# Cross-attention values as three F32R passes, and a later load of the final norm's weights, in a hybrid decoder layer

## The chip, the core and the metric

The kernel runs on one core of one Trainium2 chip. The core has five engines with instruction streams of their own: TensorE (PE; its weight loads are shown as PEld), VectorE (DVE), ScalarE (ACT), GpSimd (POOL) and SyncE (SP). SP only issues transfers here; POOL issues the transfers that add to what already stands in SBUF. Each engine takes its instructions in order. The metric is the device time of one execution in microseconds, as the median of several runs; one execution was also taken by the hardware profiler, and all lines of the profile are from that one.

## The reference

One decoder layer, `x` of 256 x 1024 in float32, with three gated branches (A: causal attention of 6 heads, B: a gated MLP that mixes tokens, C: cross attention of 4 heads into 256 memory tokens), then a final norm. What matters here is branch C and the end:

```python
def memory_cross_attention(q, mem_n, w_mem_kv):
    mk, mv = jnp.split(mem_n @ w_mem_kv, 2, axis=-1)
    ...
    lg = jnp.einsum('bshd,bmhd->bhsm', qh, kh).astype(jnp.float32) * (HEAD_DIM ** -0.5)
    p = jax.nn.softmax(lg, axis=-1).astype(q.dtype)
    return jnp.einsum('bhsm,bmhd->bshd', p, vh).reshape(B, S, C_WIDTH)
...
    out_c = memory_cross_attention(qc, mem_n, w_mem_kv[layer]) * jax.nn.silu(gc)
    y = (jax.nn.sigmoid(ma) * (out_a @ w_branch_a[layer])
         + jax.nn.sigmoid(mb) * (out_b @ w_branch_b[layer])
         + jax.nn.sigmoid(mc) * (out_c @ w_branch_c[layer]))
    x = x + y @ w_out[layer]
return rms_norm(x, final_norm_g)
```

## The kernel before

**Chunks.** The weights stream through in pieces of 128 x 1024 float32, called chunks. Each is split into a rounded high part (`split_hi`, ACT, line 264) and the rest (`split_lo`, VectorE, line 267), both in the type F32R; TensorE then makes three passes, high by high, high by low and low by high (`mm3`, lines 450 to 453). Five split chunks fit at a time (`SPL`), and a chunk is split four chunks ahead of its use (`LEAD`).

**The order of chunks** stands in `SEQUENCE` (line 52), which `plan` reads. A name such as `qc0`, `ga3` or `ub4` is a feature chunk (`mm_fea`), `w02` a branch chunk (`mm_br`, half 0, part 2), and a dot is the next product of `st`, which is two chunks of half the TensorE time each. Ahead of them come the memory's keys and values (`mm_mvk`) and a token chunk (`mm_tok`); behind them eight chunks of the output projection (`mm_out`). `n_br` is the number of chunks before those eight.

**The products of `st`** (`mm_st`) are in five groups. In a group seven products stand for eight: their left operands are sums and differences of the normed input, and their weights are sums of blocks. `ORDER` is the order of the seven, 1, 2, 5, 3, 6, 7, 4. The sums of weights are made in two buffers, `form0` and `form1`. Products 1, 2 and 3 load a block with a plain transfer from SP (`form_load`, line 231); products 5, 7 and 4 add a block onto what stands there, with a transfer from POOL (`form_add`, line 234); product 6 adds the two buffers on VectorE (`form_sum`, line 238). A transfer into a half of a buffer can go out once that half's last split is done; so 5 follows 1, 7 follows 3, 4 follows 6, 3 follows 2, and the next group's 2 and 1 follow 4 and 7.

**Plain weights** are loaded by SP, two chunks at a time, into three buffers `raw` (`load_part`, line 210).

**Everything else** is a list of units (`Units`) with an engine, a length, what each comes after, and sometimes a due chunk. Before and after every chunk `slot` issues the units that fit by a reckoned clock: one for TensorE goes out when what it needs is reckoned to be done 1.8 us before; one for another engine when that engine is reckoned free; one that is due goes out in any case. A unit without an engine, such as a load, goes out as soon as all that it comes after is issued. The order is so fixed when the kernel is built.

**Cross attention.** `evict_mv` (line 607) scales the values out of PSUM into the third part of `cx`, in float32. `join_half` makes high and low parts of the queries (`qch`, `qcl`) and keys (`mkh`, `mkl`) in the slots `och`, `sg0`, `ocl` and `sg1`. Per head h there is a chain of units: scores (`cs`, with `mm3`), the softmax (`cn`), the transpose of the probabilities and their copy to SBUF (`cp`: `c_pT` on TensorE, `c_pT_out` on ACT, line 918), then the product with the values and its copy (`cv`: `c_pv`, line 925, float32; `c_out`, line 931). `cp` of a head comes after `cv` of the head two before, `cs` after `cp` of the head three before; the six heads of branch A follow in the same row. None of these has a due chunk.

**Slots.** `slot_tile` puts a tile into a named place of SBUF; a later tile of the same name waits until all readers of the earlier one are done. `sg0` and `sg1` later hold the first gates (`sig0`, `sig1`), `ga` and `gc` the gates of branches A and C, then `ah` and a part of `al`; `ga` holds at the end the final norm's weights.

**The final norm's weights** (`load_fin`, line 771) are one transfer on SP of a row of 1024 to all 128 partitions, 512 KB. The unit `fin` comes after chunk `at_br[1, 2]`, the last that multiplies with `ah`, whose slot they take. `out_gain` (line 1140, POOL) multiplies with them in the output stage. `load_x` is issued eight chunks before the output chunks.

Of the kernel before, what the change touches and what calls it, by code (L numbers as in the profile page):

```python
# [24 lines left out]
F32 = mybir.dt.float32  # L25
F32R = mybir.dt.float32r
BF16 = mybir.dt.bfloat16
AF = mybir.ActivationFunctionType
# [5 lines left out]
S = 256  # L34
KD = D // 128
HA, GB, HC = 6, 6, 4
AW, BW, CW = 768, 768, 512
# [11 lines left out]
FAST = 5  # L49


SEQUENCE = ("qc0 . qc1 qc2 qc3 . q0 k0 . q1 . . k1 q2 . k2 q3 k3 . . q4 k4 . . q5 k5 . . ga0 ga1 . ga2 ga3 . . "
            "ga4 ga5 . . gc0 . gc1 . gc2 gc3 . ub4 ub5 . . gb4 gb5 . . w00 w01 . . w10 w11 . w02 w12 . . w03 w04 "
            ". . w05 w13 . . w14 w15 . w06 w07 . w16 w17")


# [21 lines left out]
PE, DVE, ACT, POOL, QUEUE = range(5)  # L78
# [69 lines left out]
def tile_hybrid_layer(ctx: ExitStack, tc: tile.TileContext, mw, xT, mem, x, fin_g, ln_g, w, ws, w_sp, b_sp, b_spt, rope, out):  # L148
    nc = tc.nc
# [7 lines left out]
    V = {}  # L157

    def slot_tile(name, shape, tag, dt=F32):
        V[name] = act.tile(shape, dt, name=name, tag=tag)  # L160
        return V[name]
# [16 lines left out]
    def hsl(h):  # L178
        return slice(h * 128, (h + 1) * 128)
# [17 lines left out]
    n_br = len(chunks)  # L197
# [260 lines left out]
    def sub_lo(dl, p, dh):  # L458
        nc.vector.tensor_tensor(dl, p, dh.bitcast(F32), OP.subtract)

    def later(name, e, us, fn, *args, after=(), due=10 ** 6):

        U.add(name, e, us, lambda: fn(*args), after=list(after) + [f"c{now[0]}"], first=True, due=due)
# [139 lines left out]
    def cross_tile():  # L603
        if "cx" not in V:
            slot_tile("cx", [128, 3, HC, S], "p2")

    def evict_mv():
        cross_tile()
        for t in range(2):
            h = V["cx"][:, 2, 2 * t:2 * t + 2, :].rearrange("p a b -> p (a b)")  # L610
            nc.scalar.activation(h, acc["mv", 0][t], AF.Copy, scale=rstm[:, t:t + 1])

    def evict_v(c, o):
        slot_tile("va", [128, 2, AW], "v0")
# [21 lines left out]
    def join_half(name, h, c, p):  # L636
        pa, pb = p[:, 0:S], p[:, S:2 * S]

        def join(dst):

            if name == "mk":
                U.chain(f"mk{h}", (ACT, 0.4, lambda: nc.scalar.activation(dst, pa, AF.Copy)),
                        (DVE, 0.42, lambda: nc.vector.tensor_tensor(dst, dst, pb, OP.add)), after=[f"c{c + (h > 0)}"],
                        due=(7, 9, 9, 10)[h])
                return
            nc.scalar.activation(dst, pa, AF.Copy)
            U.end[f"e{c}{h}"] = U.run(ACT, 0.4, U.end[f"c{c}"])
            later(f"{name}{h}", DVE, 0.42, lambda: nc.vector.tensor_tensor(dst, dst, pb, OP.add), after=[f"e{c}{h}"],
                  due=c + 1)

        if name in ("q", "k"):
            if name == "q" and h == 0:
                slot_tile("qk", [128, HA, 2, S], "p1")
            join(V["qk"][:, h, int(name == "k"), :])
        elif name in ("qc", "mk"):
            i = int(name == "mk")
            cross_tile()
            join(V["cx"][:, i, h, :])
            if h % 2:
                n, high, low = (("qc", "och", "sg0"), ("mk", "ocl", "sg1"))[i]  # L660
                hs = slice(h - 1, h + 1)
                u = V["cx"][:, i, hs, :]

                def hi_part():
                    if n + "h" not in V:
                        slot_tile(n + "h", [128, HC, S], high, F32R)
                        slot_tile(n + "l", [128, HC, S], low, F32R)
                    nc.scalar.activation(V[n + "h"][:, hs, :], u, AF.Copy)

                if i:  # L670
                    U.add(f"mkf{h}", DVE, 0.7, lambda: nc.vector.tensor_tensor(
                        u, u, bc["m"][:, None, :].to_broadcast([128, 2, S]), OP.mult),
                        after=[f"mk{h - 1}", f"mk{h}", "mrms"], first=True)
                U.chain(f"{name}l{h}", (ACT, 0.62, hi_part),
                        (DVE, 0.7, lambda: sub_lo(V[n + "l"][:, hs, :], u, V[n + "h"][:, hs, :])),
                        after=[f"mkf{h}"] if i else [f"qc{h - 1}", f"qc{h}", "mrow"], first=True,
                        due=10 ** 6 if i else c + 4)
        elif name == "ub":
            if h == 4:
                slot_tile("ub", [128, 2, S], "ub")  # L680
            join(V["ub"][:, h - 4, :])
        elif name in ("ga", "gc"):
            if h == 0:
                slot_tile(name, [128, HA if name == "ga" else HC, S], name)
            join(V[name][:, h, :])
        elif name == "gb":
            g = join_pair(name, h)
            join(g[:, h % 2, :])
            if h % 2:
                u = V["ub"]  # L690
                U.chain(f"gbs{h // 2}", (ACT, 0.62, lambda: nc.scalar.activation(g, g, AF.Silu)),
                        (DVE, 0.69, lambda: nc.vector.tensor_tensor(u, u, g, OP.mult)),
                        after=[f"gb{h - 1}", f"gb{h}", "exps"], due=c + 4)
# [220 lines left out]
        transpose4(ST["cp", h], [p[:, hsl(j)] for j in (0, 2, 1, 3)])  # L914

    def c_pT_out(h):
        ST["cT", h] = work.tile([128, 512], F32, name="pt", tag="pt", bufs=3)
        nc.scalar.activation(ST["cT", h], ST["cp", h], AF.Copy)

    def c_pv(h):  # L920
        p = ST["cT", h]
        mv = V["cx"][:, 2].rearrange("p (t a) b -> p t (a b)", t=2)
        ST["co", h] = ps = bank()
        for m in range(2):
            nc.tensor.matmul(ps[:, 0:S], mv[:, m, hsl(h)], p[:, m * S:(m + 1) * S], start=m == 0, stop=m == 1)

    def c_out(h):
        if "oc" not in V:
            mid_tile()
            V["oc"] = V["mid"][:, 1:3, :].rearrange("p a (b s) -> p (a b) s", b=2)  # L930
        nc.scalar.activation(V["oc"][:, h, :], ST["co", h][:, 0:S], AF.Copy)

    for h in range(HC):
        U.chain(f"cs{h}", (PE, 0.72, lambda h=h: c_scores(h)), (DVE, 0.9, lambda h=h: c_max(h)),
                (ACT, 1.15, lambda h=h: softmax_exp("c", h)),

                after=[f"qcl{h | 1}", f"mkl{h | 1}", "sqrts"] + back("p", h))
        U.chain(f"cn{h}", (DVE, 0.2, lambda h=h: softmax_sum("c", h)), (ACT, 0.85, lambda h=h: softmax_norm("c", h)),
                after=[f"cs{h}"])
        U.chain(f"cp{h}", (PE, 0.44, lambda h=h: c_pT(h)), (ACT, 0.62, lambda h=h: c_pT_out(h)), after=[f"cn{h}"] + back("v", h))  # L940
        U.chain(f"cv{h}", (PE, 0.88, lambda h=h: c_pv(h)), (ACT, 0.4, lambda h=h: c_out(h)), after=[f"cp{h}", "mve"])

    for h in range(HA):
        if h % 2 == 0:
# [110 lines left out]
    for i in range(2):  # L1055
# [2 lines left out]
              after=[f"cv{2 * i}", f"cv{2 * i + 1}", "gcs"], due=at_br[0, 0] - 6)  # L1058
        two_split(f"ocT{i}", lambda hs=hs: (V["oc"][:, hs, :], V["och"][:, hs, :], V["ocl"][:, hs, :]),
                  [f"gc_{i}", "ocTa"], due=at_br[0, 6] - 2)  # L1060
    U.add("fin", None, 0, load_fin, after=[f"c{at_br[1, 2]}"], wait=8.0)


    BR = [("a", k) for k in range(HA)] + [("b", k) for k in range(GB)] + [("c", k) for k in range(HC)]
# [270 lines left out]
```

## Time and profile before

| | us |
|---|---|
| median of three runs | 317.16 |
| lowest and highest run | 315.87, 317.94 |
| the profiled execution | 316.66 |
| its span, first to last instruction | 315.0 |

In the lines of the profile, an instruction is named by engine, source line, operation and its tiles, out<-in. In the timeline and in the chain the two first numbers are start and duration in microseconds from the start of the span; brackets at the end of a timeline row hold the idle time of the engine before it and what ended it. The table of waits gives total, number of times and the longest. A row of windows gives the stretch, its length, then busy time and number of instructions of TensorE, its weight loads, VectorE, ACT and POOL, and last the granted clock, the busy share of the 16 DMA engines and GB/s. A DMA row gives size and the median time from issue to landing. F32 products appear as two records each, so the four products of two cross heads are eight rows of line 925.

### The profile page before, as it was taken

What the parts mean: (1) busy time and instruction counts of PE and PEld (TensorE: products, weight loads), DVE (VectorE), ACT (ScalarE), POOL (GpSimd) and SP (SyncE); (2) the same over time, 40 slices, a digit from 0 to 9 for tenths busy, and PEclk for the clock granted to TensorE, in tenths of its full rate; (3) what the DMA queues carried; (4) which work ended last, traced back from release to release, by engine and by line L of the source; (5) the groups of instructions that cost most, each with busy time, mean ns of one, the idle gap of its engine ahead of it and who ended that gap; (6) DMA issues with size and microseconds to landing.
All of it is one profiled execution on the core that took longest, in us unless ns stands there. A gap on an engine that the chain in (4) does not pass through costs nothing.

```text
span 315.0 us, 4466 instructions
## 1 busy us (share of the span) xinstructions
PE 306.6 (97%) x1550; PEld 259.1 (82%) x1550; DVE 262.4 (83%) x380; ACT 229.4 (73%) x361; POOL 34.1 (11%) x55
## 2 busy tenths in 40 slices
PE   8999999999999999999999999999999998999992
PEld 4888888888888888888888888888888886888982
DVE  2869999998988898794797998999996599989532
ACT  4786998676649975969979998688758655586333
POOL 1000040040020030013013002013020031000022
PEclk9999999999999999999999999999999999999998
DMA  7999999679997559959769989779999879933003
GB/s 194 405 404 414 415 292 315 266 133 243 360 244 250 192 161 202 333 150 264 225 158 217 224 280 284 190 257 157 215 313 277 306 198 203 392 143 133 2 3 130
DMA packets 20470, 75.14 MB, mean 239 GB/s; under 512 B 2656, under 2 KB 3680, under 8 KB 18016
## 3 DMA queue, kind: packets, MB, share of 16 engines
q1 hardware_dynamic: 15984, 59.00, 52.0%
q0 software_dynamic: 4320, 15.73, 27.5%
q8 instruction: 12, 0.20, 0.2%
q10 hardware_dynamic: 144, 0.13, 0.1%
q14 instruction: 10, 0.08, 0.1%
HBM read 73.02 MB, written 1.05 MB: 235 GB/s over the span
## 4 chain that ended last, share of the span: by engine, by line
PE 82%; DMA 7%; DVE 4%; issue 3%; ACT 2%; POOL 0%; ACTq 0%; SPq 0%; POOLq 0%
PE acc L633 27%; PE acc L573 18%; DMA form<-in_ws_dram 6%; PE aux L573 6%; PE acc L511 4%; PE acc L452 3%; PE acc L451 3%; PE acc L453 3%; PE aux L505 3%; DVE lo L267 2%; PE aux L798 2%; PE acc L484 2%; PE aux L484 2%; DMA raw<-in_w_dram 2%; PE aux L453 1%
## 5 line engine op out<-in xcount | busy, mean ns | idle before, releaser
L267 DVE TENSOR_TENSOR lo<-form,hi 128x1024 fp32r<-128x1024 f32 x70 | 84.4, 1221 | 15.1 <-ACT hi L264 14.9
L264 ACT ACTIVATE hi<-form 128x1024 fp32r<-128x1024 f32 x70 | 73.0, 1056 | 26.8 <-DMA form<-in_ws_dram 11.5
L267 DVE TENSOR_TENSOR lo<-raw,hi 128x1024 fp32r<-128x1024 f32 x58 | 70.1, 1222 | 10.4 <-ACT hi L264 9.8
L264 ACT ACTIVATE hi<-raw 128x1024 fp32r<-128x1024 f32 x58 | 61.0, 1057 | 8.5 <-PE acc L453 2.6
L633 PE MATMUL acc<-n,hi 128*128 128x512 f32 x240 | 59.6, 392 | 0.0
L234 POOL DMA_DIRECT2D form<-in_ws_dram x30 | 26.1, 871 | 232.2 <-DVE lo L267 101.5
L633 PEld LDWEIGHTS acc<-n,hi 128*128 128x128 f32 x240 | 43.9, 188 | 8.4
L633 PEld LDWEIGHTS acc<-n,lo 128*128 128x128 f32 x240 | 31.6, 191 | 1.5
L633 PE MATMUL acc<-n,lo 128*128 128x256 f32 x240 | 32.8, 285 | 0.0
L573 PE MATMUL acc<-hi,s 128*128 128x512 f32 x96 | 32.8, 401 | 0.0
L573 PE MATMUL acc<-hi,n 128*128 128x512 f32 x72 | 24.2, 397 | 0.0
L573 PEld LDWEIGHTS acc<-hi,s 128*128 128x128 f32 x96 | 18.1, 188 | 3.6
L573 PE MATMUL aux<-hi,s 128*128 128x512 f32 x64 | 20.7, 390 | 0.0
L573 PE MATMUL acc<-lo,s 128*128 128x512 f32 x48 | 18.8, 391 | 0.0
L573 PEld LDWEIGHTS acc<-hi,n 128*128 128x128 f32 x72 | 13.5, 188 | 2.7
L573 PE MATMUL aux<-hi,n 128*128 128x512 f32 x48 | 15.7, 391 | 0.0
L573 PE MATMUL acc<-lo,n 128*128 128x512 f32 x36 | 14.1, 391 | 0.0
L573 PEld LDWEIGHTS aux<-hi,s 128*128 128x128 f32 x64 | 12.0, 188 | 2.4
L573 PE MATMUL aux<-lo,s 128*128 128x512 f32 x32 | 12.6, 395 | 1.2 <-DVE lo L267 1.2
L238 DVE TENSOR_TENSOR form<-form,form 128x1024 f32<-128x1024 f32 x10 | 12.2, 1221 | 0.0
L573 PEld LDWEIGHTS aux<-hi,n 128*128 128x128 f32 x48 | 9.0, 188 | 1.8
L573 PEld LDWEIGHTS acc<-lo,s 128*128 128x128 f32 x48 | 9.1, 189 | 1.6
(241 smaller groups left out, 582.4 us busy)
## 6 DMA issues: line engine op xcount, KB each, us to landing
raw<-in_w_dram SPq DMA_DIRECT2D x18, 1024.0 KB, 8.4
form<-in_ws_dram SPq DMA_DIRECT2D x30, 512.0 KB, 6.1
form<-in_ws_dram POOLq DMA_DIRECT2D x30, 512.0 KB, 7.9
raw<-in_w_dram SPq DMA_DIRECT2D x22, 512.0 KB, 8.3
st<-in_mw_dram SPq DMA_DIRECT2D x7, 384.0 KB, 7.5
raw<-in_w_dram SPq DMA_DIRECT2D x8, 256.0 KB, 7.5
xk<-in_x_dram SPq DMA_DIRECT2D x2, 512.0 KB, 7.8
xt<-in_xT_dram SPq DMA_DIRECT2D x2, 512.0 KB, 8.4
```

What stands on the lines that cost most here:

```text
L234: nc.gpsimd.dma_start(form_half(i, h), block(g, b, h), accum_op=OP.add)
L238: nc.vector.tensor_tensor(form_half(i, h), form_half(i, h), form_half(1 - i, h), OP.add)
L264: nc.scalar.activation(hi[c][:, a:b], source(c)[:, a:b], AF.Copy)
L267: nc.vector.tensor_tensor(lo[c][:, a:b], source(c)[:, a:b], hi[c][:, a:b].bitcast(F32), OP.subtract)
L451: nc.tensor.matmul(p, s_hi, m_hi, start=first, stop=False)
L452: nc.tensor.matmul(p, s_hi, m_lo, start=False, stop=False)
L453: nc.tensor.matmul(p, s_lo, m_hi, start=False, stop=last)
L484: nc.tensor.matmul(acc[name, o][t], src[:, k0 + i, tsl(t)], wt[c][:, i * 512:(i + 1) * 512], start=c == 8 and i + j == 0, stop=c == 11 and ...
L505: nc.tensor.matmul(acc["mv", 0][t][:, a:b], src[:, k, tsl(t)], wt[:, a:b], start=k + n == 0, stop=k == KD - 1 and n == len(parts) - 1)
L511: nc.tensor.matmul(p, wt, m, start=k == 0 and j < HC, stop=k == KD - 1 and j >= HC)
L573: nc.tensor.matmul(p, x[:, k0 + k, tsl(t)], wt[c][:, a * 512:(a + 1) * 512], start=first and a + j == 0, stop=half == 1 and a + j == 3, sk ...
L633: nc.tensor.matmul(o, wt, m, start=i == 0, stop=i == len(passes) - 1, skip_group_check=True)
```

## The change

1. The values of cross attention are kept as a high and a low part, `mvh` and `mvl`, in the slots `sg0` and `sg1`. ACT writes the high part with the scale; VectorE writes the low part with a unit that is due two chunks later.
2. The transposed probabilities become a high part (the copy by ACT, now F32R) and a low part (`c_pT_lo`, VectorE, new), in the slots `ub` and `v1`. `c_pv` then makes three passes per half with `mm3`. The chain `cv` has the low part as a new first unit and, as before, no due chunk; it comes after both `mvl`.
3. The low parts of queries and keys move from `sg0` and `sg1` to `gc` and `ga`. (In the code the names `high` and `low` are the slots of these two parts.)
4. In `SEQUENCE` some products of `st` change places with plain chunks.
5. The unit `fin` comes after chunk `n_br - 2`, the last but one of the branch chunks.

```diff
-SEQUENCE = ("qc0 . qc1 qc2 qc3 . q0 k0 . q1 . . k1 q2 . k2 q3 k3 . . q4 k4 . . q5 k5 . . ga0 ga1 . ga2 ga3 . . "
-            "ga4 ga5 . . gc0 . gc1 . gc2 gc3 . ub4 ub5 . . gb4 gb5 . . w00 w01 . . w10 w11 . w02 w12 . . w03 w04 "
+SEQUENCE = ("qc0 . qc1 qc2 qc3 . q0 . k0 q1 . . k1 q2 . k2 q3 k3 . . q4 k4 . . q5 k5 . . ga0 ga1 . ga2 ga3 . . "
+            "ga4 . ga5 . gc0 . . gc1 gc2 ub4 . gc3 . . . ub5 . gb4 gb5 . w00 w01 . w10 w11 . w02 w12 . . w03 w04 "
             ". . w05 w13 . . w14 w15 . w06 w07 . w16 w17")
...
     def evict_mv():
-        cross_tile()
+        for n, tag in (("mvh", "sg0"), ("mvl", "sg1")):
+            slot_tile(n, [128, 2, CW], tag, F32R)
         for t in range(2):
-            h = V["cx"][:, 2, 2 * t:2 * t + 2, :].rearrange("p a b -> p (a b)")
-            nc.scalar.activation(h, acc["mv", 0][t], AF.Copy, scale=rstm[:, t:t + 1])
+            p, f = acc["mv", 0][t], rstm[:, t:t + 1]
+            h = V["mvh"][:, t, :]
+            nc.scalar.activation(h, p, AF.Copy, scale=f)
+            later(f"mvl{t}", DVE, 0.7, scaled_lo, V["mvl"][:, t, :], p, f, h, due=now[0] + 2)
...
-                n, high, low = (("qc", "och", "sg0"), ("mk", "ocl", "sg1"))[i]
+                n, high, low = (("qc", "och", "gc"), ("mk", "ocl", "ga"))[i]
...
     def c_pT_out(h):
-        ST["cT", h] = work.tile([128, 512], F32, name="pt", tag="pt", bufs=3)
+        ST["cT", h] = work.tile([128, 512], F32R, name="pt", tag="pt", bufs=3)
         nc.scalar.activation(ST["cT", h], ST["cp", h], AF.Copy)
 
+    def c_pT_lo(h):
+        if h < 2:
+            slot_tile(f"ptl{h}", [128, 512], ("ub", "v1")[h], F32R)
+        sub_lo(V[f"ptl{h % 2}"], ST["cp", h], ST["cT", h])
+
     def c_pv(h):
-        p = ST["cT", h]
-        mv = V["cx"][:, 2].rearrange("p (t a) b -> p t (a b)", t=2)
+        p, low = ST["cT", h], V[f"ptl{h % 2}"]
         ST["co", h] = ps = bank()
         for m in range(2):
-            nc.tensor.matmul(ps[:, 0:S], mv[:, m, hsl(h)], p[:, m * S:(m + 1) * S], start=m == 0, stop=m == 1)
+            ms = slice(m * S, (m + 1) * S)
+            mm3(ps[:, 0:S], V["mvh"][:, m, hsl(h)], V["mvl"][:, m, hsl(h)], p[:, ms], low[:, ms], m == 0, m == 1)
...
-        U.chain(f"cv{h}", (PE, 0.88, lambda h=h: c_pv(h)), (ACT, 0.4, lambda h=h: c_out(h)), after=[f"cp{h}", "mve"])
+        U.chain(f"cv{h}", (DVE, 0.68, lambda h=h: c_pT_lo(h)), (PE, 0.72, lambda h=h: c_pv(h)), (ACT, 0.4, lambda h=h: c_out(h)),
+                after=[f"cp{h}", "mvl0", "mvl1"])
...
-    U.add("fin", None, 0, load_fin, after=[f"c{at_br[1, 2]}"], wait=8.0)
+    U.add("fin", None, 0, load_fin, after=[f"c{n_br - 2}"], wait=8.0)
```

## The prediction, made before the changed kernel had run

> **What bounds the kernel now.** I read the page first: busy time, the slices, the shares of the chain that ended last.
>
> ```profile
> PE 306.6 (97%) x1550; PEld 259.1 (82%) x1550; DVE 262.4 (83%) x380; ACT 229.4 (73%) x361; POOL 34.1 (11%) x55
> ...
> PE   8999999999999999999999999999999998999992
> ...
> DVE  2869999998988898794797998999996599989532
> ...
> PE 82%; DMA 7%; DVE 4%; issue 3%; ACT 2%; POOL 0%; ACTq 0%; SPq 0%; POOLq 0%
> ```
>
> TensorE is busy in every slice but the first, the last and one near 265 us. Time can therefore be won in only two ways: fewer or shorter products, or the closing of a hole. VectorE, at 83% and at nine tenths in most slices, is the second scarce engine, and the change gives it work. The chain of work in order of time says where the hole comes from, and the timeline of TensorE how long it is.
>
> ```profile
> 232.50 0.83 POOL form L234
> ...
> 234.80 12.19 DMA form<-in_ws_dram
> 247.09 1.07 ACT hi L264
> ...
> 260.53 1.23 DVE lo L267
> 261.80 1.42 PE aux L573 x5
> ```
>
> ```profile
> 261.80 0.50 PE L573 MATMUL aux<-lo,s 128*128 128x512 f32 x1 [1.16 <-DVE lo L267]
> ```
>
> An accumulating transfer from POOL, issued at 234.80, lands 12.19 us later; only then can ACT round that chunk (247.09), VectorE works its backlog off from there, and the split at 260.53 ends after TensorE wants it: a hole of 1.16 us. What that transfer shared the DMA engines with is in SP's timeline, the table of waits, the windows and the DMA issues:
>
> ```profile
> 229.27 1.46 SPq L231 DMA_DIRECT2D form<-in_ws_dram  x2
> 234.28 0.33 SPq L773 DMA_DIRECT2D fing<-in_fin_g_dram  x1
> 234.66 0.73 SPq L210 DMA_DIRECT2D raw<-in_w_dram  x1
> 242.11 1.46 SPq L231 DMA_DIRECT2D form<-in_ws_dram  x2
> ```
>
> ```profile
> SPq L773 <- PE acc L453: 3.7, 1, 3.7
> ```
>
> ```profile
> 235.00:247.00 12.00, 12.00 (x54) 9.95 (x53) 6.65 (x7) 7.58 (x9) 0.66 (x1) 1.00 1.00 287
> ```
>
> ```profile
> form<-in_ws_dram SPq DMA_DIRECT2D x30, 512.0 KB, 6.1
> form<-in_ws_dram POOLq DMA_DIRECT2D x30, 512.0 KB, 7.9
> ...
> fing<-in_fin_g_dram SPq DMA_DIRECT2D x1, 512.0 KB, 8.8
> ```
>
> The reader is to see that the final norm's weights (`fing`) are fetched at 234.28, half a microsecond before the late transfer, that the DMA engines are full from 235 to 247 (share 1.00 at 287 GB/s), and that SP stood 3.7 us in front of this fetch, waiting for the products with `ah`, with a load of branch weights behind it.
>
> **The change, part by part.**
>
> *The products.* A cross head's values take two F32 products of 256 columns. The chain has them at 0.86 us a head (first and last of four rows). They become six F32R passes; those of the cross scores are the same shape.
>
> ```profile
> 114.16 0.86 PE aux L925 x4
> ...
> 136.65 0.87 PE aux L925 x4
> ```
>
> ```profile
> 90.26 0.28 PE L451 MATMUL aux<-mkh,qch 128*128 128x256 f32 x1
> ...
> 92.29 0.28 PE L453 MATMUL aux<-mkh,qcl 128*128 128x256 f32 x1
> ```
>
> From 90.26 to 92.29 eighteen passes start, 17 steps of 0.119 us. Six take 0.72 us, so a head gains 0.865 - 0.716 = 0.15 and four gain 0.59 us, all on the path, as TensorE has no hole there. The Trainium skill ("FP8 and Floating Point Precision", TensorE Precision Notes) says that true FP32 takes four passes through the array. By that, three passes would save a quarter of 0.865 us a head, 0.87 us in all; the row gives less, because a 256-column F32R pass takes 0.119 us here and not a quarter of 0.43 (0.108).
>
> *The low parts.* Four differences of 128x512 out of PSUM and two scaled ones are new on VectorE. Nearest rows:
>
> ```profile
> 186.86 0.68 DVE L589 TENSOR_TENSOR sig<-sig,acc 128x512 f32<-128x512 f32 x1
> ...
> 194.19 0.48 DVE L987 SCALAR_TENSOR_TENSOR ut<-aux,b_col,ut 128x256 f32<-128x256 f32 x1
> ```
>
> 4 x 0.68 = 2.7 us, and for the scaled ones 2 x 0.75 = 1.5 us (between 0.68 and twice 0.48; nearer the first, since most of 0.48 is a start that is paid once). ACT's work stays: the eviction and the copy of the transposed probabilities only change their type. What covers the 1.5 us, near 54 us: the tightest chunks behind it had their low part done at 67.93, and TensorE began them at 69.28, the second product of this row:
>
> ```profile
> 65.43 2.50 DVE L267 TENSOR_TENSOR lo<-form,hi 128x1024 fp32r<-128x1024 f32 x2
> ```
>
> ```profile
> 69.05 0.62 PE L573 MATMUL acc<-hi,s 128*128 128x512 f32 x2
> ```
>
> For the first of the two that is 69.28 - 66.65 = 2.6 us of lead; 1.5 us fit, cost nothing. The 2.7 us lie between 111 and about 140:
>
> ```profile
> 110.00:120.00 10.00, 10.00 (x60) 8.84 (x60) 9.51 (x12) 7.34 (x13) 3.46 (x4) 1.00 0.64 161
> 120.00:130.00 10.00, 10.00 (x56) 8.70 (x55) 7.71 (x23) 7.04 (x19) 0.00 (x0) 1.00 1.06 226
> ```
>
> ```profile
> 130.28 1.23 DVE L267 TENSOR_TENSOR lo<-raw,hi 128x1024 fp32r<-128x1024 f32 x1 [0.79 <-ACT hi L264]
> ```
>
> ```profile
> 133.61 2.09 PE L633 MATMUL acc<-n,hi 128*128 128x512 f32 x8
> ```
>
> VectorE idles 2.8 us in those twenty, and the tightest chunk (ga2, done 131.51, used 133.61) has 2.1 us. I take nothing; if the idle time can't be used, 2.7 - 2.1 = 0.6 us is the other end.
>
> *The wait that is added.* `c_pv` on TensorE now waits for VectorE's `c_pT_lo`. Behind it on TensorE stand the next chunk's products, and ACT's `c_out` waits for it. The planner issues it only 1.8 us after it reckons the low part done. I take nothing; the dear end is one split (1.22 us) ahead of each low part that the planner doesn't see, 4.9 us for four.
>
> *The new places in SBUF.* `mkl` moves to where `ga` comes later, `qcl` to `gc`, the value halves to `sg0` and `sg1`, the probabilities' low parts to `ub` and `v1`. The shortest distance is that of `mkl`:
>
> ```profile
> 115.33 0.28 PE L452 MATMUL aux<-mkl,qch 128*128 128x256 f32 x1
> ...
> 130.15 0.36 ACT L646 ACTIVATE ga<-acc 128x256 f32<-128x256 f32 x1
> ```
>
> Some 14.5 us lie between its last reader and the next writer: nothing, until the scores slip by that much.
>
> *`SEQUENCE`.* One product of group 0, and later the products 5 and 6 of group 2, 4 of group 2 and 1, 2, 5, 3 of group 3, come one to three places forward (a place, of 2.73 us, is two chunks of `st` or one other chunk). The tight spot: 4 of group 2 and 1, 2 of group 3 now stand in a row, with one chunk before 5. Product 2's load refills what product 4 read two places earlier, not four; product 5's accumulation goes onto product 1 three places later, not four.
>
> ```profile
> 184.59 2.35 DVE L267 TENSOR_TENSOR lo<-form,hi 128x1024 fp32r<-128x1024 f32 x2
> ...
> 188.66 1.22 DVE L267 TENSOR_TENSOR lo<-form,hi 128x1024 fp32r<-128x1024 f32 x1
> ```
>
> ```profile
> 191.39 0.58 PE L573 MATMUL acc<-hi,n 128*128 128x512 f32 x1
> ...
> 195.12 0.48 PE L573 MATMUL aux<-hi,n 128*128 128x512 f32 x1
> ```
>
> Product 4's first half is split at 185.8 and used at 191.39, 5.6 us ahead; product 1's at 189.9 and 195.12, 5.2 ahead. With such leads, product 2 has 5.6 + 2 x 2.73 = 11.0 us and needs 6.1 (load) + 2.3 (rounding 1.06 and split 1.22) + about 1 of queueing: 1.6 us over. Product 5 has 5.2 + 3 x 2.73 = 13.4 and needs 7.9 + 2.3 + 1.3: 1.9 over. Cost nothing; the dear end is an accumulation of 12.19 instead of 7.9 us, 4.3 - 1.9 = 2.4 us of hole. Later products of group 3 get more room.
>
> *The fetch of `fing`.* It leaves 234.28 and is emitted in front of the last branch chunk's products, behind SP's last load but one. SP's wait of 3.7 us goes with it, since `ah` is long free there; so the branch weights behind it are issued earlier.
>
> ```profile
> 269.19 14.08 SPq L210 DMA_DIRECT2D raw<-in_w_dram  x3
> ```
>
> ```profile
> 302.40 1.29 POOL L1140 TENSOR_TENSOR xk<-xk,fing 128x512 f32<-128x512 f32 x1 [39.43 <-ACT jk L1136]
> ```
>
> SP's last three weight loads spread from 269.19 to 283.27, so the fetch goes out near 278 and, at 8.8 us, lands near 287, some 15 us before POOL reads it: free there. What it leaves behind: 0.52 MB at 287 GB/s is 1.83 us of full DMA engines ahead of the late transfer. TensorE comes 0.59 us sooner by the products, so the hole would be 1.75 us; 1.83 us earlier closes it. Gain 1.16 us; the other end is 0, if the bytes don't matter. What is late next is nothing below 1 us that I can see.
>
> **The sum** is -0.59 - 1.16 = -1.75 us. The profiled execution took 316.66 us (span 315.0 and 1.66 around it): 314.9. The median of the three runs, 317.16, lies 0.5 above it, so I say 315.4.
>
> **The rivals.**
> *A, the fetch doesn't matter* (that part doesn't do what it may). For it: the accumulation runs on POOL's queue, the fetch on SP's, and the branch weights, freed of the 3.7 us, now push in earlier. Against it: 287 GB/s with a share of 1.00, so bytes are what is short. The hole stays; 317.16 - 0.59 = 316.6. The Trainium skill ("DMA: Bandwidth & Descriptors", Queues, rings and completion order) has each DMA engine take turns between the queues by packets; by that alone the accumulation speeds up only once SP's queue is empty, which fits this rival as well as the forecast.
> *B, slower: three products in a row starve.* Place: products 2 and 5 of group 3, near 195 us. For it: leads shrink to 3 or 4 us elsewhere, and the margins above are under 2 us. Against it: the nearest accumulations took about the 7.9. From 9.8 us on there is a hole, from 11.5 it eats the whole gain; at 12.19, 317.16 - 1.75 + 2.4 = 317.8.
> *C, TensorE waits for the new low parts.* For it: VectorE at 9.51 of 10 where the first two fall. Against it: TensorE waits nowhere there now on similar chains. At half its dear end, 317.16 - 1.75 + 2.45 = 317.9.
> *D, three of four passes.* A quarter of the products' time: 317.16 - 0.87 - 1.16 = 315.1; the row of 0.119 us speaks against it.
>
> **How the numbers follow.** Forecast 0.50, A 0.20, B 0.16, C 0.09, D 0.05. The time is 315.4. The three runs spread from 315.87 to 317.94, some 0.7 us to either side of a median, so the forecast's own range is 314.6 to 316.2. Down to 314.2 it takes in D; up to 317.9 it takes in A and the price of B and half of that of C, leaving some 2 in 10 outside. A measurement of this kernel tells about 1% from no change: 314.0 and 320.3. Below 314.0 the sum can't go without a hole that I don't see, 0.06; above 320.3 only C at its full price or B and C together, 0.06; within, 0.88.
>
> **What would show it.** Products: six passes at 0.12 us a head in place of 0.86. Fetch: the transfer that took 12.19 us lands in about 10, and the hole before 261.80 is gone; if it stays, A. Row of three: no idle TensorE near 195; if some, B, with ACT waiting for a `form` transfer. Low parts: no idle TensorE between 111 and 140; if some, C. A hole at a place not named here would make the prediction wrong altogether, as would a shift of all stages through the planner, whose order I did not follow unit by unit.

## The result, and the profile after

The changed kernel takes 318.42 us (median of 19 runs, 316.46 to 320.65), the kernel before 316.69 on the same chips (19 runs). The ratio is 1.0059, with an interval of 1.0041 to 1.0076: about 1.9 us slower, where 1.75 us faster was forecast. Times here and below are medians of all executions, the ratios follow the means without executions over 1.5% above the fastest of their kernel, and so the two can differ by up to half a per cent. The profiled execution has a span of 317.8 us against 315.0.

The page of the changed kernel: busy times, the slices of TensorE and VectorE, the shares of the chain.

```profile
PE 307.0 (97%) x1558; PEld 258.7 (81%) x1558; DVE 265.5 (84%) x386; ACT 228.7 (72%) x361; POOL 35.9 (11%) x55
...
PE   8999999999999999999999999998999998999992
...
DVE  2969999899988896999697886999797599989532
...
PE 67%; DMA 12%; DVE 9%; issue 8%; ACT 2%; POOL 1%; SPq 0%; ACTq 0%; POOLq 0%; DVEq 0%
```

TensorE's share of the chain fell from 82% to 67%; transfers, VectorE and issue time took its place. What TensorE waited for is in the table of waits, and where, in its timeline:

```profile
PE aux L573 <- DVE lo L267: 2.2, 3, 1.2
PE aux L990 <- DVE mt L1007: 1.3, 1, 1.3
```

```profile
123.34 0.28 PE L451 MATMUL aux<-pt,mvh 128*128 128x256 f32 x1
...
123.94 0.28 PE L453 MATMUL aux<-pt,mvl 128*128 128x256 f32 x1
...
199.86 0.50 PE L573 MATMUL aux<-lo,s 128*128 128x512 f32 x1 [0.43 <-DVE lo L267]
...
218.12 1.10 PE L990 MATMUL aux<-vb,wsp 128*128 128x256 f32 x4 [1.25 <-DVE mt L1007]
...
241.53 0.39 PE L573 MATMUL aux<-hi,n 128*128 128x512 f32 x1
...
252.30 0.50 PE L573 MATMUL aux<-lo,s 128*128 128x512 f32 x1 [0.64 <-DVE lo L267]
...
264.64 0.50 PE L573 MATMUL aux<-lo,s 128*128 128x512 f32 x1 [1.16 <-DVE lo L267]
```

Behind the start there are four holes where there was one. The old one, before 261.80, is still there with its 1.16 us, at 264.64; new are 0.43, 1.25 and 0.64 us before 199.86, 218.12 and 252.30. The three new ones sum to 2.3 us; with 0.2 us or so at each restart (in the experiments below, two holes of 1.00 and 0.38 us lengthen the stretch between the same two products by 1.73 us) and 0.4 us more at the start of this execution, less 0.59 for the products, it is about the 2.8 us of the two spans.

The chain of work of the changed kernel leads to the holes:

```profile
187.87 9.54 DMA form<-in_ws_dram
197.48 1.07 ACT hi L264
198.58 1.24 DVE lo L267
199.86 1.43 PE aux L573 x5
...
239.15 10.68 DMA form<-in_ws_dram
```

The accumulation for product 5 of group 3 (in the row of three) takes 9.54 us, and TensorE waits: that is rival B's place, at a sixth of its price. The accumulation that took 12.19 us now takes 10.68, as the moved fetch should bring, but it is issued at 239.15, and not at 234.80. TensorE at that stage is 2.0 us later than it was: the product that starts at 241.53 above is this one of the kernel before:

```profile
239.53 0.39 PE L573 MATMUL aux<-hi,n 128*128 128x512 f32 x1
```

So the transfer is issued 4.35 - 2.0 = 2.35 us later against TensorE, and lands 4.35 - 1.51 - 2.0 = 0.84 us later against it, though it is quicker. The 2.35 us can be read off VectorE's stream, here of the changed kernel with POOL's row, and below of the kernel before:

```profile
228.84 1.22 DVE L267 TENSOR_TENSOR lo<-raw,hi 128x1024 fp32r<-128x1024 f32 x1
229.97 1.28 DVE L1019 TENSOR_TENSOR obl<-aux,obh 128x512 fp32r<-128x512 f32 x2
231.17 1.28 DVE L1019 TENSOR_TENSOR ocl<-mid,och 128x512 fp32r<-128x512 f32 x2
232.37 2.35 DVE L267 TENSOR_TENSOR lo<-form,hi 128x1024 fp32r<-128x1024 f32 x2
...
239.15 0.86 POOL L234 DMA_DIRECT2D form<-in_ws_dram  x1 [1.47 <-DVE lo L267]
```

```profile
226.89 1.22 DVE L267 TENSOR_TENSOR lo<-raw,hi 128x1024 fp32r<-128x1024 f32 x1
228.02 2.35 DVE L267 TENSOR_TENSOR lo<-form,hi 128x1024 fp32r<-128x1024 f32 x2
```

The split at 228.84 is still as early against TensorE as the one at 226.89. But then four low parts of left operands of branches B and C (`obl`, `ocl`, 2.4 us) stand ahead of the splits of form chunks, and POOL waits for a later one of these; in the kernel before they were done earlier. The planner put them there.

The holes at 199 and 218 have another history, in the windows of the changed kernel, and below of the kernel before (VectorE's busy time is the third pair of numbers):

```profile
190.00:200.00 10.00, 9.57 (x47) 7.76 (x46) 6.11 (x6) 7.05 (x10) 0.00 (x0) 1.00 1.01 308
200.00:210.00 10.00, 10.00 (x54) 8.53 (x55) 9.90 (x11) 10.00 (x17) 0.91 (x2) 1.00 0.58 207
210.00:220.00 10.00, 8.75 (x42) 7.12 (x42) 10.00 (x14) 5.38 (x6) 2.57 (x3) 1.00 1.03 251
```

```profile
190.00:200.00 10.00, 10.00 (x52) 8.52 (x51) 8.94 (x14) 8.92 (x13) 1.73 (x2) 1.00 0.89 228
200.00:210.00 10.00, 10.00 (x57) 8.67 (x56) 9.46 (x13) 7.12 (x10) 0.00 (x0) 1.00 0.79 247
210.00:220.00 10.00, 10.00 (x45) 8.27 (x45) 9.28 (x11) 7.87 (x10) 3.48 (x4) 1.00 0.84 184
```

Between 190 and 200 VectorE works 6.1 us instead of 8.9: the DMA engines are full (share 1.01) and the next chunks have not come; as its stream is in order, the gates and mixes behind those splits stand too. From 200 to 220 it has next to no free moment (19.9 of 20), and TensorE's mixes wait for it at 218. From the first feature product (39 us) to 199 TensorE's timeline shows no hole; VectorE's low parts and the products they feed make none in this kernel, where the planner put the products of head 0 at 123.34 instead of 114.16.

The new instructions have the forecast sizes (groups of the changed kernel, busy time and mean in ns): six passes start within 0.60 us above, a pitch of 0.12, and

```profile
L459 DVE TENSOR_TENSOR ptl<-aux,pt 128x512 fp32r<-128x512 f32 x4 | 2.7, 684 | 0.0
L456 DVE SCALAR_TENSOR_TENSOR mvl<-aux,rstm,mvh 128x512 fp32r<-128x512 f32 x2 | 1.5, 745 | 0.0
```

### The profile page after: what moved, and what is told of

The parts are those of the page before. It is cut to its first block, busy times and chain, and to the rows that moved or that the text cites. A ratio compares the mean times of both kernels' runs of the same rounds, so it can differ in the third digit from the quotient of the medians.

```text
span 317.8 us, 4488 instructions
## 1 busy us (share of the span) xinstructions
PE 307.0 (97%) x1558; PEld 258.7 (81%) x1558; DVE 265.5 (84%) x386; ACT 228.7 (72%) x361; POOL 35.9 (11%) x55
## 4 chain that ended last, share of the span: by engine, by line
PE 67%; DMA 12%; DVE 9%; issue 8%; ACT 2%; POOL 1%; SPq 0%; ACTq 0%; POOLq 0%; DVEq 0%
PE acc L636 22%; PE acc L573 15%; DMA form<-in_ws_dram 10%; DVE lo L267 5%; PE aux L505 3%; PE acc L511 3%; PE acc L451 3%; PE acc L452 3%; PE acc L453 3%; PE aux L573 3%; DMA st<-in_mw_dram 2%; PE aux L452 2%; PE aux L453 2%; PE aux L451 2%; PE aux L484 2%
## 5 line engine op out<-in xcount | busy, mean ns | idle before, releaser
L573 PE MATMUL acc<-hi,s 128*128 128x512 f32 x96 | 31.8, 396 | 0.0
```

The lines of the kernel that those rows point to most:

```text
L573: nc.tensor.matmul(p, x[:, k0 + k, tsl(t)], wt[c][:, a * 512:(a + 1) * 512], start=first and a + j == 0, stop=half == 1 and a + j == 3, sk ...
```

## The experiments

All ratios are against runs of the kernel before on the same chip; the kernel before took 316.2 to 316.6 us in the five groups. The theories are named in the expectations. What they and the prediction call products 5 and 6 of group 2 are by `ORDER` and the dots of `SEQUENCE` its products 2 and 6.

**The fetch and the order, alone and taken back.** Edits, in turn: the kernel before with the new place of the fetch; the kernel before with the new `SEQUENCE`; the changed kernel with the old place of the fetch; the changed kernel with the low part right behind its copy, and the planner told of it.

```diff
# fetch alone (and, reversed, fetch taken back)
-    U.add("fin", None, 0, load_fin, after=[f"c{at_br[1, 2]}"], wait=8.0)
+    U.add("fin", None, 0, load_fin, after=[f"c{n_br - 2}"], wait=8.0)
# order alone: both changed lines of SEQUENCE
# low part at once, in c_pT_out
         nc.scalar.activation(ST["cT", h], ST["cp", h], AF.Copy)
+        c_pT_lo(h)
+        U.end[f"cp{h}"] = U.run(DVE, 0.7, U.t[ACT])
...
-        U.chain(f"cv{h}", (DVE, 0.68, lambda h=h: c_pT_lo(h)), (PE, 0.72, lambda h=h: c_pv(h)), ...
+        U.chain(f"cv{h}", (PE, 0.72, lambda h=h: c_pv(h)), ...
```

> The kernel before with the fetch of the final norm's weights moved alone. Theory H (late heads: the undated low parts hold the cross heads back, the gates' work slides into the crowded stretch behind 200 us): the fetch is innocent and closes the hole of 1.16 us at 261.8, so 1.0 to 1.2 us under the kernel before. Theory F (the fetch: freed of its wait, SP pushes branch weights in ahead of the accumulations): no gain, 0 to 1 us over the kernel before, and the transfer of 12.2 us no shorter.

> The kernel before with the new order of chunks alone. Theory S (the order: three products in a row starve): the holes of the changed kernel near 199, 216 and 251 us appear here too, 2 to 3 us over the kernel before. Theory H: at most the one near 199, 0 to 0.7 us over, and none at 216 or 251.

> The changed kernel with the fetch back where it was. Theory F: the holes near 251 and 263 us shrink, 1 us or more under the changed kernel. Theories H and S: the accumulation shares with the fetch again, 0 to 1.2 us over the changed kernel.

> The changed kernel, with each head's low part of the probabilities issued right behind its high part and not as a unit of its own. Theory H: the product with the values of head 0 comes near 114 us in place of 123, the gates' work returns to before 200, the holes at 216 and 251 go: 2 to 3.5 us under the changed kernel, 315 to 316.5. Theory S: the holes stay, within 0.5 us of the changed kernel, 318 to 318.9.

| | us | ratio |
|---|---|---|
| fetch alone | 315.35 | 0.9961 (0.9942 to 0.9979) |
| order alone | 319.67 | 1.0088 (1.0060 to 1.0117) |
| changed, fetch taken back | 320.73 | 1.0128 (1.0094 to 1.0162) |
| changed, low part at once | 323.36 | 1.0170 (1.0114 to 1.0226) |

The fetch does what the prediction says. In the kernel with it alone the hole is gone and the chain is TensorE's, as its page shows:

```profile
PE 96%; DMA 2%; ACT 1%; ACTq 0%; SPq 0%; issue 0%; DVE 0%
```

Its gain of 1.2 us is there in the changed kernel as well: taken back, it costs some 2.2 us (1.0128 against 1.0059). So theory F falls. The order alone costs 2.8 us, the size that theory S gave it and about that of the whole change or more (the intervals overlap). But it has none of the holes near 199, 216 and 251 that S asked for; its table of waits has

```profile
PE aux L573 <- DVE lo L267: 1.4, 2, 1.2
PE acc L633 <- DVE gc L648: 1.4, 1, 1.4
```

The second is new: a feature chunk at 180 waits for a PSUM bank that VectorE's half of an eviction (`gc`) still reads, behind two splits. And theory H's cure, earlier low parts, makes it worse, where S had no change. There a form chunk comes late, ACT stands for it, and the copy that frees a PSUM bank stands behind it (ACT's timeline, then TensorE's waits):

```profile
122.65 1.06 ACT L264 ACTIVATE hi<-form 128x1024 fp32r<-128x1024 f32 x1 [4.20 <-DMA form<-in_ws_dram]
123.61 0.36 ACT L941 ACTIVATE mid<-aux 128x256 f32<-128x256 f32 x1
```

```profile
PE aux L992 <- DVE ut L998: 2.2, 1, 2.2
PE aux L838 <- ACT mid L941: 1.3, 1, 1.3
```

**The passes under the old order, and the order's two late halves.** The first two kernels have the low part at once, as above, and the old `SEQUENCE`, with the old and the new place of the fetch; the other two are the kernel before with a part of the new order. The undated low parts were not tried with the old order. The two halves are not the whole late part: the full order also has `ub4` in front of `gc3`, and neither half has that.

```diff
# first half of the late part (products 2, 6 of group 2)
-            "ga4 ga5 . . gc0 . gc1 . gc2 gc3 . ub4 ub5 . . gb4 gb5 . . w00 w01 . . w10 ...
+            "ga4 . ga5 . gc0 . . gc1 gc2 gc3 . ub4 ub5 . . gb4 gb5 . . w00 w01 . . w10 ...
# second half (the row of three)
+            "ga4 ga5 . . gc0 . gc1 . gc2 gc3 . ub4 . . . ub5 . gb4 gb5 . w00 w01 . w10 ...
```

> The kernel before with the three passes alone: old order of chunks, old place of the fetch of fing, and the low part of the probabilities made right behind its copy. Theory Q (the passes are worth what the row of 0.119 us says, VectorE's 4.2 us are covered): 316.6 - 0.6 = 316.0 us, ratio 0.998, no new idle TensorE before 250 us, the hole of 1.3 near 261 stays. Theory V (VectorE's new low parts move its other work, and that costs a hole elsewhere): 317.2 us or more, ratio 1.002 to 1.010, with a hole of over 0.5 us behind 111 us that the kernel before does not have.

> As the kernel with the passes alone, and with the late fetch of fing: the whole change without its new order of chunks. Theory Q: the gains add, 315.35 - 0.6 = 314.8 us, ratio 0.994. Theory S (the order alone is what made the changed kernel slower): the same, and at any rate under 316, some 3 us under the changed kernel's 318.4. Theory V: 317 us or more, TensorE idle behind 111 us.

> The kernel before with only the first half of the late part of the new order: products 5 and 6 of group 2 are taken forward among ga5, gc0 and gc1; product 4 of group 2 and group 3 stay where they were. Theory R (the row of three products, 4 of group 2 and 1, 2 of group 3, starves VectorE): no change, 316.5 us, ratio 0.999 to 1.002. Theory G (products 5, 6 of group 2 ahead of gc1, gc2 hold up the gates' evictions and VectorE, the hole near 178 us): 318 us or more, ratio 1.004 to 1.010, and VectorE idle for over 2 us between 165 and 180.

> The kernel before with only the second half of the late part of the new order: products 4 of group 2 and 1, 2 of group 3 in a row, with ub5 and gb4, gb5 behind. Theory R: the cost of the order is here, 318.5 to 319.5 us, ratio 1.006 to 1.010: VectorE waits for transfers for over 3 us between 185 and 205 where it had 1.1 in the kernel before, works that off until about 220, the accumulation for group 4 is issued some 2 us later against TensorE, and holes lie near 200 or 250 and 262. Theory G: no change, 316.5 us. If both halves are without effect, the cost comes from their sum or from the early change at q1, and both theories fall.

| | us | ratio |
|---|---|---|
| passes, low part at once | 324.96 | 1.0252 (1.0198 to 1.0305) |
| the same with the fetch | 323.12 | 1.0190 (1.0137 to 1.0242) |
| order of group 2 | 319.72 | 1.0124 (1.0075 to 1.0174) |
| the row of three | 317.33 | 1.0036 (1.0016 to 1.0057) |

Theory V holds in its direction, far beyond the size that it asked for: the passes alone, with the low part at once, cost 2.5%, some 8 us, and with the fetch 1.9%, so that Q and S fall. (In the profiled execution of the first, 5.4 us are holes, and TensorE ran at half clock for 6.8 us, of the kind that the last section shows.) With the low part at once the new order makes no difference that shows: 1.0170 in the changed kernel, 1.0190 without it. The row of three, which the prediction picked as the tight spot, costs 1.1 us; the other half of the order, to which it gave no price, costs 3.9 (3.5 by the medians). So theory G has the dearer half. Its wait is again that for `gc`:

```profile
PE acc L633 <- DVE gc L648: 2.5, 1, 2.5
```

The halves add up to 1.6%, and the whole order costs 0.9%. As the whole has the exchange of `ub4` and `gc3` and the early change besides, this hints that the price of a place depends on what else moves, and does not show it.

**Work or planner.** In the kernels with the passes the planner was told of them, and it placed every later unit anew. Here it is told nothing: lengths and dependencies are those of the kernel before, the new instructions are written out where their input is made, and on every engine all other instructions stand in the old order.

```diff
 def evict_mv():
...
-            later(f"mvl{t}", DVE, 0.7, scaled_lo, V["mvl"][:, t, :], p, f, h, due=now[0] + 2)
+            scaled_lo(V["mvl"][:, t, :], p, f, h)
...
         nc.scalar.activation(ST["cT", h], ST["cp", h], AF.Copy)
+        c_pT_lo(h)
...
-        U.chain(f"cv{h}", (DVE, 0.68, ...), (PE, 0.72, ...), (ACT, 0.4, ...), after=[f"cp{h}", "mvl0", "mvl1"])
+        U.chain(f"cv{h}", (PE, 0.88, ...), (ACT, 0.4, ...), after=[f"cp{h}", "mve"])
```

> The kernel before with the three passes alone, and the order of every other instruction on every engine just as before: the two low parts of the values stand behind their eviction, each low part of the probabilities behind its copy, and the planner is told of none of them (lengths and dependencies as in the kernel before). Old order of chunks, old fetch. Theory P (the loss of the passes is the planner's: units of other length and dependency slide all later work into other places): 316.3 - 0.6 = 315.7 us, ratio 0.998, no new hole behind 30 us. Theory W (the 4.2 us of work on VectorE, or the wait of the products for it, are what costs): over 317.5 us, ratio 1.004 or more, the hole of 1.5 to 2 us near 122 us as in the run with the passes alone.

> The same with the late fetch of fing. Theory P: both gains add, 315.35 - 0.6 = 314.8 us, ratio 0.994, the fastest of all. Theory W: over 316.5 us.

> The kernel before with the new order of chunks and the late fetch, without the passes: what the changed kernel has beside them. Theory O (the order alone is the loss, and the passes give their 0.6 us there too): 318.4 + 0.6 = 319 us, ratio 1.007 to 1.009. Theory P: the passes, as planned, cost here too; without them at most 317.6 us, ratio 1.003 or less. About the changed kernel's 318.4 would leave the passes at nothing.

> The whole change, with the planner told of none of the new low parts: every other instruction in the order of the run with new order and fetch alone. Theory P: that run less 0.6 us. Theory W: that run and 1 us or more. Theory O asks only that this and that run are both above 317.5 us.

| | us | ratio |
|---|---|---|
| frozen passes | 317.50 | 1.0033 (1.0014 to 1.0052) |
| frozen passes, fetch | 316.81 | 1.0011 (0.9999 to 1.0023) |
| order, fetch, no passes | 318.49 | 1.0077 (1.0046 to 1.0109) |
| order, fetch, frozen passes | 320.44 | 1.0141 (1.0108 to 1.0174) |

Same work, same old order of chunks: 1.0033 with the other instructions in their old order, 1.0252 where the planner placed them anew. The planner's placing, here with the low part at once, is worth about 7 us; the work itself about 1. P (0.998) misses the frozen kernel, and W (1.004 or more) lies within its interval; with the fetch, 316.81 us is where W has it (over 316.5). Its timeline of TensorE and VectorE says why:

```profile
115.16 0.68 DVE L459 TENSOR_TENSOR ptl<-aux,pt 128x512 fp32r<-128x512 f32 x1
...
115.90 0.39 PE L452 MATMUL aux<-ptl,mvh 128*128 128x256 f32 x1 [1.00 <-DVE ptl L459]
...
117.23 0.68 DVE L459 TENSOR_TENSOR ptl<-aux,pt 128x512 fp32r<-128x512 f32 x1
...
117.96 0.39 PE L452 MATMUL aux<-ptl,mvh 128*128 128x256 f32 x1 [0.38 <-DVE ptl L459]
```

The products of heads 0 and 1 wait 1.0 and 0.38 us for low parts that stand behind splits and form sums. That is rival C's mechanism, in two heads of four. Under the new order the frozen passes cost 2.0 us (1.0141 against 1.0077), again as W has it, and the same two holes are there, of 0.98 and 0.36 us. But the changed kernel (1.0059) is no slower than order and fetch without any passes (1.0077; the intervals overlap): under the new order the passes as planned cost nothing that can be measured, and order and fetch without them already lose as much.

**The wait taken away; parts of the order undone inside the changed kernel.** First the frozen passes with the fetch, and only the products of heads 0 and 1, with their copies, two half products later:

```diff
 def c_pv(h):
+    if h < 2:
+        pend.append((h, now[0] + 2))
+    else:
+        c_pv_now(h)
...
+        flush(c)    # behind the products of chunk c: c_pv_now and c_out_now of what is due
         U.slot(c, True)
```

Then the changed kernel with products 2 and 6 of group 2 at their old places; with the row of three undone (in both, `gc3` is also back in front of `ub4`); and with the early change (`q0 . k0 q1`) undone.

> The frozen passes with the late fetch (old order of chunks), and only this moved: the products of heads 0 and 1 with the values, and ACT's copies of their results, go out two half products of st (2.7 us) later. Theory T (TensorE's waits of 1.2 and 0.5 us for the low parts are all that the passes cost): no idle TensorE between 110 and 125 us, 316.8 - 1.7 = 315.1 us or a little less, ratio 0.994 to 0.996. Theory W (VectorE's 4.2 us cost in another place too): 316 us or more, ratio 0.998 or more, and a hole behind 125 us.

> The changed kernel, with products 5 and 6 of group 2 back at their old places; the row of three products (4 of group 2, 1 and 2 of group 3) stays, and the early change too. Theory G (the change among group 2 is the dear one): 315.5 to 317 us, ratio at most 1.002, no hole of over 0.5 us between 170 and 225. Theory R (the row is the dear one here, as the hole at 199 and VectorE's 3.9 us without work before it suggest): as the changed kernel, 318 to 319 us, ratio 1.005 to 1.009.

> The changed kernel with the row undone: 4 of group 2 and group 3 at their old places, products 5 and 6 of group 2 forward as in the change. Theory G: 318 to 320 us, ratio 1.005 to 1.012. Theory R: 315.5 to 317 us, no hole near 199. If this and the run with the row alone are both slow, the planner's new placing of all units under the undated low parts is what costs, and neither half.

> The changed kernel with only the early change of the order undone (q1's chunk behind the product again). Both theories: no effect, within 0.3% of the changed kernel's ratio of 1.006, since no hole before 190 us was seen there. Below 1.002 both theories fall: the early change would be what moves the later units.

| | us | ratio |
|---|---|---|
| frozen passes, fetch, heads 0 and 1 later | 314.97 | 0.9957 (0.9939 to 0.9975) |
| changed, only the row | 320.79 | 1.0136 (1.0103 to 1.0169) |
| changed, only group 2 | 324.49 | 1.0248 (1.0218 to 1.0278) |
| changed, without the early change | 318.79 | 1.0071 (1.0046 to 1.0097) |

With the products moved, the wait is gone, and 1.7 us with it (0.9957 against 1.0011): theory T. In the changed kernel, undoing either half, and the exchange with it, makes it slower, so G and R fall both; by the words of the expectation the planner's new placing is then what costs, and neither half. The early change is without effect, as both expected. With the row undone, one mix of tokens waits longer than all holes of the changed kernel together:

```profile
PE aux L990 <- DVE mt L1007: 6.5, 1, 6.5
```

It is the wait of 218.12 again. `mix_tok` needs a PSUM bank that an earlier mix holds until VectorE's `mix_bias`, which stands behind splits and form sums.

**Do the passes pay when nothing waits?** The fetch alone and the late heads with the fetch once more, on one chip.

> The kernel before with the late fetch alone, once more, on the same chip as the next one. All theories: 0.994 to 0.998, about 315.3 us.

> The late fetch with the frozen passes and the late heads, once more. Theory T (the passes give 0.6 us when nothing waits): 0.6 us under the fetch alone, in the median and in the span of the profile. Theory W' (VectorE's 4.2 us take part of it back): between 0.3 us under it and 0.3 above.

315.35 us, 0.9975 (0.9960 to 0.9991), for the fetch alone, and 315.22, 0.9969 (0.9956 to 0.9982), with the passes: no difference that the runs can tell, and by the medians theory W'. The traces can tell one, as they leave out the start, which differs by some tenths between executions. First feature product and last product of the fetch alone, and then of the late heads:

```profile
38.83 1.98 PE L633 MATMUL acc<-n,hi 128*128 128x512 f32 x8
...
307.24 0.28 PE L453 MATMUL aux<-hi,y 128*128 128x256 f32 x1
```

```profile
39.05 1.98 PE L636 MATMUL acc<-n,hi 128*128 128x512 f32 x8
...
307.02 0.28 PE L453 MATMUL aux<-hi,y 128*128 128x256 f32 x1
```

From the one to the other it is 268.41 and 267.97 us: the passes win 0.44 us of the 0.59. The earlier runs of the same two kernels have 268.41 and 267.95 us between the same two products.

## Why the prediction was wrong

**`SEQUENCE` at nothing: this step failed.** It was to cost 0 with a dear end of 2.4 us; alone it costs 2.8, and on top of the fetch 1.0077 against 0.9961, some 3.7 us. The leads of products 2 and 5 were worked out about right (0.43 us short, where 1.9 over was reckoned with a transfer of 7.9 us and it took 9.54). But these leads were the wrong question. The step followed the products that move (and took product 2 of group 2 for its product 5) and held every unit around them fixed. The planner reads the same order, and laid other units anew: in the changed kernel four low parts came to stand in front of the splits for which an accumulation waits, 2.35 us, and with the order alone a feature chunk waits 1.4 us for a gate's eviction. That is the caveat in the last sentence of the prediction, and it had no price in the sum and no rival. How much a placing can cost shows best at the passes: 7 us between two kernels that differ in the placing alone.

**The low parts and the added wait at nothing.** Their sizes were right (0.684 and 0.745 against 0.68 and 0.75), the second with some luck: from 0.48 us at 256 columns and 0.745 at 512 some 0.21 us do not grow with the columns, which is less than half of 0.48 and not most of it. The cover held for the splits: no chunk between 111 and 140 came late. The wait had a real price, though, in the kernel whose order is frozen (1.4 us, a good quarter of the 4.9), and the planner escaped it in the changed kernel by sending the products of head 0 9 us later. So the undated unit had no wait there; it had a new place.

**The products** came as forecast, at 0.12 us a pass, and 0.44 of 0.59 us where nothing else moves.

**The fetch** was right in mechanism and in size: -1.2 us alone (-0.8 in the second group of runs), the hole closed, and the transfer of 12.19 us landing in 10.5. In the changed kernel the accumulation is quicker too (10.68 for 12.19) and the gain is still there against the kernel with the fetch taken back, but the hole comes back since the accumulation is issued 2.35 us later.

**The rivals.** A fell with the fetch alone. B had a right place and too much at it (0.43 us for 2.4), and missed the half of the order that costs more. C showed itself only where the planner was kept from acting. D fell with the pitch of the passes. The range was narrow, too: the three runs lie 1.3 us below and 0.8 above their median, and not 0.7 to either side; but the sum missed by 3 us.

**What stays open.** Whether this order of chunks loses in itself, or only under this planner's placing, isn't settled: each `SEQUENCE` that was run was also placed anew. Nor was the changed kernel run with the whole old order, so that it would gain without the new one isn't shown; and the exchange of `ub4` and `gc3` was not tried by itself. That VectorE's idle time between 190 and 200 leads to the hole at 218, and the four low parts to those at 252 and 264, is read from the traces and not tried by itself. The version that is ahead of both kernels is the late fetch in the old order, without the passes, or with them where the other instructions are kept in their order and heads 0 and 1 go out later.

## What to carry to other kernels

Where a planner lays the instruction streams from lengths and dependencies, a new unit of 0.7 us is not a cost of 0.7 us: compare the streams of all engines before and after, and forecast from the difference, or fix the old streams and insert the new work by hand. Freeze everything else when a part is to be measured; here that turned a loss of 2.5% into one of 0.3%, whose wait could then be seen and removed. And ask of each engine in order what stands behind its next wait: here evictions that free PSUM banks stood behind splits that waited for transfers.

## What the runs showed of the hardware

TensorE's clock fell to half after a hole of 2.5 us. Windows of 1 us from the profiled execution of the kernel with the order of group 2, whose wait for `gc` ended at 181.47 (the granted clock is the number behind POOL's):

```profile
181.00:182.00 1.00, 0.53 (x4) 0.54 (x5) 1.00 (x4) 1.00 (x4) 0.00 (x0) 1.00 0.93 270
182.00:183.00 1.00, 1.00 (x8) 0.91 (x7) 1.00 (x2) 1.00 (x2) 0.00 (x0) 0.97 0.92 262
183.00:184.00 1.00, 1.00 (x4) 0.79 (x3) 0.97 (x3) 0.47 (x1) 0.00 (x0) 0.50 0.73 193
...
186.00:187.00 1.00, 1.00 (x5) 0.84 (x4) 0.42 (x1) 1.00 (x2) 0.00 (x0) 0.82 0.97 291
```

It is full for 1.5 us after the restart, then half for some 3.4 us, so this hole cost about 1.7 us more than its length. That execution took 322.36 us, and the other three of this kernel 319.40 to 319.74, so in those the hole was probably shorter, or the clock did not fall. The shortest single hole with half clock behind it is that of 2.2 us in the changed kernel with the low part at once, which ended at 220.01:

```profile
221.00:224.00 3.00, 3.00 (x9) 2.35 (x8) 2.79 (x6) 0.69 (x2) 0.00 (x0) 0.51 0.70 134
```

The hole of 1.9 us in the passes with the fetch left it at 1.00 (its row in the table of waits, and the window behind it):

```profile
PE aux L838 <- ACT mid L941: 1.9, 1, 1.9
```

```profile
124.00:131.00 7.00, 6.48 (x37) 5.76 (x38) 6.70 (x16) 5.96 (x13) 0.00 (x0) 1.00 1.06 259
```

The Trainium skill ("TensorE: Matmul & The Clock Gate", Part 1: The HAM clock gate) has the clock at half after an idle window of about 3.4 us, and at full again after a busy one of that length. The half rate and the 3.4 us of its length agree; that it takes 3.4 us of idle time doesn't: 2.2 us were enough here.
